# Half of the z gates ahead of the convolution units in a two-block network, step columns inside a quarter of the gates

## The chip, the cores and the metric

The kernel runs on one core of a Trainium2 chip. The metric is the device time of one launch in microseconds (us).

## What is computed

A network of two blocks over 1024 tokens of 1024 channels. The first (a linear recurrence beside differential attention, then an expert-choice feed-forward layer) is not touched. The second block begins with one wide projection; cut to what matters here:

```
h = layer_norm(x, ln_emb_g, ln_emb_b)
proj = einsum('bld,de->ble', h, w_in)
xs, z, bm, cm, dt_raw, glu, cgate = split(proj, ...)   # 1024, 1024, 256, 256, 16, 2048, 1024 columns
xbc = silu(causal_depthwise_conv(concat([xs, bm, cm]), ssm_conv_w, ssm_conv_b))       # 4 taps
dt = softplus(dt_raw + dt_bias)
y = ssd_chunked(xh, dt, a, bm_c, cm_c) + d_skip * xh
yz = y * silu(z)                                       # then a grouped rms norm: y_ssm
u = glu[..., :1024] * sigmoid(glu[..., 1024:])
u = causal_depthwise_conv(u, conf_conv_w, conf_conv_b)                                # 31 taps
u = silu(layer_norm(u, conf_ln_g, conf_ln_b))
y_conf = u * silu(cgate)
out = concat([y_ssm, y_conf]) @ w_out + b_out          # and two more norms and a gate
```

## The kernel before

Products are made at more than one pass: each operand is split into a high and a low part, and `mm3` (line 135) issues three matmuls, high by high, high by low, low by high. The contraction runs over eight tiles of 128 channels. A projection (`proj`) gives 128 columns for all 1024 tokens, with the weights stationary: 48 matmuls of 512 tokens. The gates z are wanted with tokens on partitions: `z(q)` makes 256 columns at a time for two token blocks of 128, with the tokens stationary, in 192 matmuls of 256 columns a quarter, and stores silu(z) in device memory.

A scheduler of the framework fixes the order of each engine's instructions when the program is built; the Python order of the stages, the buffers of the pools and the lists `later` and `bgq` steer it. `after()`, called at the end of every projection, runs what was put on `later`: the turning (transposing) of a finished tile on TensorE, or the sums of the step columns. `bg(us)` takes that much VectorE work from `bgq`, the queue of convolution taps: 20 of a tile's 31 taps go to VectorE (line 1295, accumulator in PSUM), the rest to ScalarE (products, line 1291) and GpSimd (additions, line 1292).

The second block's stages come in this order: the layer norm of x, read from device memory after the first block (`normed`), four token blocks at a time; their transposes (`turned`), between the matmuls of the first gated linear unit (`first`); `glu` 1; `bc` 0 (B, with its turns, line 1357); `glu` 2; `dts`, the projection of the 16 step columns (48 matmuls with 16 rows of output, line 1402 turns them); `bc` 1; `glu` 3 to 7 with `xs` 0 to 3 between; z quarters 0 to 2; the eight convolution gates (cgate); z quarter 3 with the first part of the state-space stage. `steps` makes softplus of the step columns: a chain of 15 operations on 128x128 tiles on VectorE (`log1p`, lines 179 to 188, then lines 1411 and 1416), and the matmuls of `sums` (lines 1423, 1424), which wait for it, are put three calls of `after` later:

```
later.append(lambda: later.append(lambda: later.append(sums)))
```

The norm over channels takes the mean `mu` (channel sum by TensorE, line 1488, then line 1492) late in z quarter 2; squares are summed (lines 1497, 1505); `deviation` (lines 1509 to 1515) follows behind gate 1; `gated(j)` (lines 1497, 1519, 1521) is run two gates behind the gate that it needs.

## Time and profile before

| | us |
|---|---|
| median of 3 runs (2226.93 to 2230.64) | 2229.42 |
| the profiled execution | 2233.63 |
| its span, first to last instruction | 2231.9 |
| TensorE busy | 2077.4 (93%) |
| VectorE busy | 1767.3 (79%) |
| ScalarE busy | 1200.1 (54%) |
| GpSimd busy | 515.8 (23%) |

Busy time is the time in which an engine had an instruction under way; matmuls are pipelined, so their durations overlap, and what a matmul costs is read from the distance of two starts. PE is TensorE (PEld its weight loads), DVE VectorE, ACT ScalarE, POOL GpSimd, SP SyncE, whose queue issues most transfers. All times in the rows are in us from the start of the span. The mean granted clock of TensorE is 0.964 of its full speed.

### The profile page before, as it was taken

Reading aid. Unit: us, or ns where it says so; the run is one execution under the profiler, and the core shown is the slowest. Engines: PE = TensorE matmul, PEld = TensorE weight load, DVE = VectorE, ACT = ScalarE, POOL = GpSimd, SP = SyncE. Lnnn points to the kernel's source line nnn. Section 1 sums busy time; section 2 is a strip of 40 time slices with the busy share of each in tenths; the row PEclk is TensorE's granted clock in tenths of the full one; section 3 lists DMA queues with packets and bytes.
Section 4 is the critical chain, followed back from the end, with each engine's and each line's share of the span. In section 5 each row is a group of like instructions: output and inputs, shape, how many; then the busy total and the mean of one; then the engine's idle time right before and its main releaser. Section 6 shows DMA issues by size and latency. Waiting matters only on the chain.

```text
span 2231.9 us, 27077 instructions
## 1 busy us (share of the span) xinstructions
PE 2077.4 (93%) x10214; PEld 1717.7 (77%) x10214; DVE 1767.3 (79%) x2389; ACT 1200.1 (54%) x1427; POOL 515.8 (23%) x254
## 2 busy tenths in 40 slices
PE   6989899989979999999998689989999999998997
PEld 6768678978868888878877477767889887776885
DVE  7587859976878999989977648999993748877676
ACT  5563839982327777766766447544543346544111
POOL 0133310000021121201101018766774210003000
PEclk9999999999979999999999899989999999999998
DMA  8444456127578999999998321133434458556211
GB/s 271 141 148 127 123 142 121 55 91 253 191 283 327 387 389 386 378 384 356 383 335 292 112 60 49 57 104 114 123 114 151 169 180 284 180 199 215 76 67 66
DMA packets 232802, 439.67 MB, mean 197 GB/s; under 512 B 46656, under 2 KB 134976, under 8 KB 232544
## 3 DMA queue, kind: packets, MB, share of 16 engines
q1 hardware_dynamic: 217184, 396.00, 51.3%
q0 software_dynamic: 9728, 35.66, 5.1%
q10 hardware_dynamic: 5760, 6.29, 0.8%
q8 instruction: 80, 1.31, 0.2%
q14 instruction: 50, 0.41, 0.1%
HBM read 370.74 MB, written 67.16 MB: 196 GB/s over the span
## 4 chain that ended last, share of the span: by engine, by line
PE 52%; issue 7%; DVE 6%; DMA 3%; ACT 2%; POOL 1%; SPq 0%; DVEq 0%; POOLq 0%; ACTq 0%
PE big L142 16%; PE big L139 16%; PE big L140 16%; PE tr L1012 1%; DVE tr L1295 1%; DMA x1d<-y,idx 1%; ACT wH L129 1%; PE tr L997 1%; DMA ptd<-rs 1%; DMA wr<-in_w_out_dram 1%; PE big L1357 1%; PE tr L1768 1%; POOL acc L1292 0%; DVE wL L133 0%; DVE aL L133 0%
## 5 line engine op out<-in xcount | busy, mean ns | idle before, releaser
L129 ACT CAST wH<-wr 128x2048 fp32r<-128x2048 f32 (+2 forms) x267 | 443.1, 1667 | 258.7 <-PE big L142 154.1
L133 DVE TENSOR_TENSOR wL<-wr,wH 128x2048 fp32r<-128x2048 f32 (+1 forms) x206 | 454.4, 2216 | 72.4 <-ACT wH L129 71.7
L139 PE MATMUL big<-hH,wH 128*128 128x512 f32 (+1 forms) x720 | 285.8, 402 | 11.3 <-ACT B L410 4.7
L140 PE MATMUL big<-hL,wH 128*128 128x512 f32 (+1 forms) x720 | 286.7, 400 | 6.5 <-DVE hL L326 5.7
L142 PE MATMUL big<-hH,wL 128*128 128x512 f32 (+1 forms) x720 | 228.1, 395 | 0.0
L1295 DVE SCALAR_TENSOR_TENSOR tr<-u,cols,tr 128x1024 f32<-128x1024 f32 x160 | 205.8, 1286 | 12.1 <-ACT tr L1283 8.5
L133 POOL TENSOR_TENSOR wL<-wr,wH 128x1024 fp32r<-128x1024 f32 (+2 forms) x62 | 154.7, 2501 | 253.0 <-ACT wH L129 232.7
L1292 POOL TENSOR_TENSOR acc<-acc,tmp 128x1024 f32<-128x1024 f32 x72 | 174.1, 2419 | 37.1 <-ACT tmp L1291 31.7
L139 PEld LDWEIGHTS big<-hH,wH 128*128 128x128 f32 (+1 forms) x720 | 137.3, 191 | 44.6 <-ACT B L410 5.1
L140 PEld LDWEIGHTS big<-hL,wH 128*128 128x128 f32 (+1 forms) x720 | 137.6, 191 | 38.1 <-DVE hL L326 6.8
L142 PEld LDWEIGHTS big<-hH,wL 128*128 128x128 f32 (+1 forms) x720 | 136.6, 190 | 30.8
L139 PE MATMUL big<-hH,aH 128*128 128x512 f32 x384 | 154.6, 403 | 5.3 <-ACT aH L129 2.3
L139 PE MATMUL big<-wH,0H 128*128 128x512 f32 x384 | 151.9, 395 | 3.8 <-ACT 0H L129 3.8
L139 PE MATMUL big<-wH,hH 128*128 128x256 f32 (+1 forms) x448 | 150.0, 336 | 4.6 <-ACT wH L129 2.1
L140 PE MATMUL big<-hL,aH 128*128 128x512 f32 x384 | 152.7, 398 | 1.0 <-DVE hL L1562 1.0
L140 PE MATMUL big<-wL,0H 128*128 128x512 f32 x384 | 153.1, 399 | 0.0
L140 PE MATMUL big<-wL,1H 128*128 128x512 f32 x384 | 152.3, 397 | 0.0
L139 PE MATMUL big<-wH,1H 128*128 128x512 f32 x384 | 151.1, 394 | 1.1 <-ACT 1H L129 1.1
L140 PE MATMUL big<-wL,hH 128*128 128x256 f32 (+1 forms) x448 | 149.4, 334 | 0.9 <-POOL wL L133 0.9
L142 PE MATMUL big<-wH,hL 128*128 128x256 f32 (+1 forms) x448 | 148.7, 332 | 0.0
L142 PE MATMUL big<-wH,0L 128*128 128x512 f32 x384 | 120.3, 395 | 4.8 <-DVE 0L L133 4.7
L142 PE MATMUL big<-hH,aL 128*128 128x512 f32 x384 | 122.9, 398 | 1.8 <-DVE aL L133 1.5
(534 smaller groups left out, 4470.4 us busy)
## 6 DMA issues: line engine op xcount, KB each, us to landing
wr<-in_w_dram SPq DMA_DIRECT2D x192, 1024.0 KB
wr<-in_w_in_dram SPq DMA_DIRECT2D x48, 512.0 KB
wm<-in_w_mod_dram SPq DMA_DIRECT2D x32, 512.0 KB
wm<-in_w_mod_dram SPq DMA_DIRECT2D x8, 1024.0 KB
wr<-in_w_in_dram SPq DMA_DIRECT2D x32, 256.0 KB
u<-ucd SPq DMA_DIRECT2D x16, 512.0 KB
wr<-in_w_out_dram SPq DMA_DIRECT2D x14, 512.0 KB
hL<-in_x_dram SPq DMA_DIRECT2D x8, 512.0 KB
```

The source lines that it names most:

```text
L129: self.high = nc.scalar.copy(h, src)
L133: (le or nc.vector).tensor_sub(l, src, h)
L139: mm(o, aH, bH, start=start, stop=False)
L140: mm(o, aH, bL, start=False, stop=False)
L142: mm(o, aL, bH, start=False, stop=stop)
L997: self.turn = nc.tensor.matmul(pr[:, 0:4], oh[:, b], tk[:, e, b], start=b == 0, stop=b == NB - 1)
L1012: self.turned = nc.tensor.transpose(pt[:, k * P:(k + 1) * P], src[:, k * P:(k + 1) * P], self.ident)
L1292: nc.gpsimd.tensor_add(part[0], part[0], tmp)
L1295: nc.vector.scalar_tensor_tensor(acc[0], u[:, t:t + S], w(t), acc[0], op0=ALU.mult, op1=ALU.add)
L1357: nc.tensor.transpose(pt[:, b], src[:, b * P:(b + 1) * P], self.ident)
L1768: nc.tensor.transpose(pt[:, k * P:(k + 1) * P], src[:, k * P:(k + 1) * P], self.ident)
```

## The change

The second block begins with the first half of z instead of the first unit: its 512 gate columns are made for two token blocks at a time (`tokens`, `gates`), 48 matmuls of 512 columns each, and the layer norm and the transposes go by two token blocks too (`normed`, `turned`); the square root there is made on VectorE alone (`rsqrt_v`). `glu(0)` is a unit like the others. `dts` makes z's third quarter, 256 columns, with the 16 step columns beside it, in 192 matmuls of 272 columns; `steps` has no turning any more, its bias is added as a row, and `sums` is put one call of `after` later instead of three. Behind `glu(7)` come gates 0 to 2 in place of z quarters 0 to 2; `mu` follows gate 2, `deviation` gate 4, and gates 4 and 5 have buffers of their own. The last z quarter stays where it was.

```diff
-        self.w0 = self.c_weights(W[:, 2576:2576 + P], W[:, 3600:3600 + P], le=self.nc.vector)
-        self.x0 = self.normed(0, [self.ct(i // 2) for i in range(4)])
-
-    def normed(self, half, xts):
-
-        nc, sm = self.nc, self.csm
+        self.w0 = self.z_weights(W[:, 1024:1536], le=self.nc.vector)
+        ln = lambda n, *w: self.cst.tile([P, NB, *w], F, name="ln" + n)
+        self.lnv, self.lnr, self.lnb = ln("v", 2), ln("r"), ln("b")
+        self.rows = {p: self.normed(p) for p in range(2)}
...
+    def normed(self, p):
+
+        nc, sm, mv = self.nc, self.csm, self.lnv
+        xts = [self.ct(p % 2) for _ in range(2)]
         for i, xt in enumerate(xts):
-            b = half * 4 + i
+            b = p * 2 + i
             self.xload = nc.sync.dma_start(xt, self.x1d[b * P:(b + 1) * P, :])
-        mv = sm.tile([P, 4, 2], F, name="mv")
-        r = sm.tile([P, 4], F, name="cer")
-        nm = sm.tile([P, 4], F, name="nm", bufs=1)
-        for p in range(2):
-            for i in (2 * p, 2 * p + 1):
-                bs = sm.tile([P, 2, 6], F, name="bs")
-                for q in range(2):
-                    nc.vector.bn_stats(bs[:, q], xts[i][:, q * 512:(q + 1) * 512])
-                nc.vector.bn_aggr(mv[:, i], bs.rearrange("p a b -> p (a b)"))
-            ps = slice(2 * p, 2 * p + 2)
-            self.rsqrt(sm, mv[:, ps, 1], 2, 1.0, LN_EPS, "ce", r[:, ps])
-            if half == 0:
-                nc.vector.scalar_tensor_tensor(nm[:, ps], mv[:, ps, 0], -1.0, r[:, ps], op0=ALU.mult, op1=ALU.mult)
-            for i in (2 * p, 2 * p + 1):
-                if half == 0 and i % 2 == 0:
-                    nc.scalar.activation(xts[i], xts[i], AF.Identity, bias=nm[:, i:i + 1], scale=r[:, i:i + 1])
-                else:
-                    self.last = nc.vector.tensor_scalar(xts[i], xts[i], mv[:, i, 0:1], r[:, i:i + 1], op0=ALU.subtract, op1=ALU.mult)
-        return xts, mv, r
+        bs = slice(2 * p, 2 * p + 2)
+        for i, xt in enumerate(xts):
+            st = sm.tile([P, 2, 6], F, name="bs")
+            for q in range(2):
+                nc.vector.bn_stats(st[:, q], xt[:, q * 512:(q + 1) * 512])
+            nc.vector.bn_aggr(mv[:, 2 * p + i], st.rearrange("p a b -> p (a b)"))
+        r = self.lnr[:, bs]
+        nc.vector.tensor_copy(r, self.rsqrt_v(sm, mv[:, bs, 1], 2, 1.0, LN_EPS, "ce"))
+        nc.vector.scalar_tensor_tensor(self.lnb[:, bs], mv[:, bs, 0], -1.0, r, op0=ALU.mult, op1=ALU.mult)
+        b = 2 * p
+        nc.scalar.activation(xts[0], xts[0], AF.Identity, bias=self.lnb[:, b:b + 1], scale=r[:, 0:1])
+        nc.vector.tensor_scalar(xts[1], xts[1], mv[:, b + 1, 0:1], r[:, 1:2], op0=ALU.subtract, op1=ALU.mult)
+        return xts
+
+    def z_weights(self, *aps, le=None):
+
+        nc, wp = self.nc, self.cwp
+        ws = []
+        for h in range(4):
+            wr = self.cwr.tile([P, 2, 512], F, name="wr")
+            n = 0
+            for ap in aps:
+                n += ap.shape[1]
+                nc.sync.dma_start(wr[:, :, n - ap.shape[1]:n], ap[h * 256:(h + 1) * 256].rearrange("(k p) n -> p k n", p=P))
+            wH = wp.tile([P, 2, 512], R, name="wH")
+            wL = wp.tile([P, 2, 512], R, name="wL")
+            self.split(wH[:, :, 0:n], wL[:, :, 0:n], wr[:, :, 0:n], le or nc.gpsimd)
+            ws += [(wH[:, k, 0:n], wL[:, k, 0:n]) for k in range(2)]
+        return ws
...
+        def turned(p, xts):
+
+            ts = slice(p * 256, p * 256 + 256)
+            for k4 in range(2):
+                pt = (pq.tile([P, 4, 256], F, name="big") if k4 else pt1.tile([P, 4, 256], F, name="tr"))
+                for q in range(4):
+                    k = k4 * 4 + q
+                    for i in range(2):
                         nc.tensor.transpose(pt[:, q, i * P:(i + 1) * P], xts[i][:, k * P:(k + 1) * P], self.ident)
+                for q in range(4):
+                    k = k4 * 4 + q
                     g, b = self.col("ln_emb_g", k), self.col("ln_emb_b", k)
-                    nc.scalar.activation(hH[k][:, hs], pt[:, q], AF.Identity, bias=b, scale=g)
-                    if half:
+                    nc.scalar.activation(hH[k][:, ts], pt[:, q], AF.Identity, bias=b, scale=g)
+                    if p == 0 or q == 3:
                         nc.vector.tensor_scalar(pt[:, q], pt[:, q], g, b, op0=ALU.mult, op1=ALU.add)
                     else:
-                        self.evac = nc.scalar.activation(pt[:, q], pt[:, q], AF.Identity, bias=b, scale=g)
-                    nc.vector.tensor_sub(hL[k][:, hs], pt[:, q], hH[k][:, hs])
+                        nc.scalar.activation(pt[:, q], pt[:, q], AF.Identity, bias=b, scale=g)
+                    nc.vector.tensor_sub(hL[k][:, ts], pt[:, q], hH[k][:, ts])
...
+        def tokens(p, w, mid=None):
+
+            ps = pq.tile([P, 2, 512], F, name="big")
+            n = w[0][0].shape[1]
+            for kt in range(KT):
+                if kt == 4 and mid:
+                    mid()
+                for i in range(2):
+                    sl = slice((p * 2 + i) * P, (p * 2 + i + 1) * P)
+                    self.mm3([ps[:, i, 0:n]], hH[kt][:, sl], hL[kt][:, sl], [w[kt][0]], [w[kt][1]], kt == 0, kt == KT - 1)
+            after()
+            return ps
+
+        def gates(p, ps, c0, n):
+
+            o = st.tile([P, 2, n], F, name="t2", bufs=3)
+            nc.scalar.activation(o, ps[:, :, 0:n], AF.Silu)
+            nc.sync.dma_start(self.szd[p * 256:(p + 1) * 256, c0:c0 + n].rearrange("(a p) c -> p a c", p=P), o)
...
+            turned(0, self.rows.pop(0))
+
+            def mid(p):
+                if p < 3:
+                    turned(p + 1, self.rows.pop(p + 1))
+                if p < 2:
+                    self.rows[p + 2] = self.normed(p + 2)
+
+            for p in range(4):
+                gates(p, tokens(p, w, lambda: mid(p)), 0, 512)
...
-            ps = proj(weights(W[:, 2560:2576]), 0, NE)
-            raw = st.tile([NE, S], F, name="t2", bufs=3)
-            nc.scalar.activation(raw, ps[0:NE, :], AF.Identity, bias=self.col("dt_bias")[0:NE])
-            later.append(lambda: steps(raw))
...
+            db = sm.tile([P, NE], F, name="db")
+            self.row_bcast(db, "dt_bias")
+            w = self.z_weights(W[:, 1536:1792], W[:, 2560:2576])
             cut = Cut(ct(1))
             v = cut.tile([P, P], F, "v")
-            nc.scalar.copy(v, pt[:, 0])
+            for p in range(4):
+                ps = tokens(p, w)
+                gates(p, ps, 512, 256)
+                nc.vector.tensor_add(v[:, p * 32:p * 32 + 32].rearrange("p (b h) -> p b h", b=2), ps[:, :, 256:272],
+                                     db[:, None, :].to_broadcast([P, 2, NE]))
+                self.bg(10.0)
+            steps(cut, v)
...
-            later.append(lambda: later.append(lambda: later.append(sums)))
-
-        def z_weights(q):
-            return weights(W[:, 1024 + q * 256:1280 + q * 256])
-
-        def z(q, w=None, mid={}):
-
-            cs = slice(q * 256, (q + 1) * 256)
-            w = w or z_weights(q)
+            later.append(sums)
...
+        def cgate(j):
+            if j % 2 == 0:
+                self.wc = weights(W[:, 4624 + j * P:4880 + j * P])
+            ps = proj(self.wc, j % 2)
+            os[j] = self.cp.tile([P, S], F, name="os", bufs=2) if j in (4, 5) else ct(j % 2)
+            nc.scalar.activation(os[j], ps, AF.Silu)
+
+        first(self.w0)
...
-        z(0)
-        z(1)
+        cgate(0)
+        cgate(1)
...
-        z(2, mid={ZM: [lambda: nc.scalar.activation(mu, chan_sum(s1, mu), AF.Copy, scale=1.0 / D)]})
+        cgate(2)
+        nc.scalar.activation(mu, chan_sum(s1, mu), AF.Copy, scale=1.0 / D)
...
-        os = {}
-        for j in range(KT):
-            if j % 2 == 0:
-                w = weights(W[:, 4624 + j * P:4880 + j * P])
-            ps = proj(w, j % 2)
-            os[j] = ct(j % 2)
-            nc.scalar.activation(os[j], ps, AF.Silu)
-            if j == 1:
+        for j in range(3, KT):
+            cgate(j)
+            if j == 4:
                 deviation()
-            if j > 1:
-                gated(j - 2, os.pop(j - 2))
-        w = z_weights(3)
-        for j in (6, 7):
+            if j >= 4:
+                for i in range(j - 1 if j > 4 else 0, j):
+                    gated(i, os.pop(i))
+        w = weights(W[:, 1792:2048])
+        for j in sorted(os):
             gated(j, os.pop(j))
         es1.close()
         self.c2_es.close()
         es.close()
         self.ssd_open()
         mid, first = self.ssd_first(pq)
-        z(3, w, mid)
+        z(w, mid)
```

The order of TensorE around the sums of the step columns, before (L1423, L1424; `t` is the product of step and decay, `hH` and `hL` the split tokens, `wH` and `wL` the split weights):

```order
L140 MATMUL big<-hL_10518,wH 128x512
L139 MATMUL big<-hH_10510,wH 128x512
L140 MATMUL big<-hL_10518,wH 128x512
L142 MATMUL big<-hH_10510,wL 128x512 x2
L1423 MATMUL big<-t_11475,iota_10325 128x128
L1424 MATMUL big<-t_11475,ones 128x128
L139 MATMUL big<-hH_10503,wH 128x512
```

The same place now (lines are one less or some ten more):

```order
L138 MATMUL big<-wH,hH_10521 128x272
L139 MATMUL big<-wL,hH_10521 128x272
L141 MATMUL big<-wH,hL_10529 128x272
L138 MATMUL big<-hH_10514,wH 128x512
L139 MATMUL big<-hL_10522,wH 128x512
...
L139 MATMUL big<-hL_10529,wH 128x512
L141 MATMUL big<-hH_10521,wL 128x512 x2
L1434 MATMUL big<-t_11655,iota_10325 128x128
L1435 MATMUL big<-t_11655,ones 128x128
L138 MATMUL big<-hH_10514,wH 128x512
```

Between the turned step columns and the sums 144 matmuls stood (three projections); now 48 (one) stand between the quarter's last matmul and the sums.

VectorE in the first part of the step chain, before (L179 to L187 are the chain, L1295 the taps, L1350 those of the short convolution, L1298 the end of a tile's convolution):

```order
L179 TENSOR_SCALAR t_11475<-t_11475 128x128
L1350 SCALAR_TENSOR_TENSOR t_11499<-big,cols,t_11499 128x1021
L1295 SCALAR_TENSOR_TENSOR tr<-u,cols,tr 128x1024
L180 RECIPROCAL t_11475<-t_11475 128x128
L1298 TENSOR_TENSOR acc<-tr,acc 128x1024
L1339 MEMSET u 128x30
L181 TENSOR_TENSOR t_11475<-t_11475 128x128
L183 TENSOR_TENSOR t_11475<-t_11475 128x128
L185 TENSOR_SCALAR t_11475<-t_11475 128x128
```

The same place now (L178 to L186 are the chain, L1314 the taps, L1410 the added bias of the last two token blocks):

```order
L1410 TENSOR_TENSOR t_11655<-big,db 128x32
L1314 SCALAR_TENSOR_TENSOR tr<-u,cols,tr 128x1024
L178 TENSOR_SCALAR t_11655<-t_11655 128x128
L1314 SCALAR_TENSOR_TENSOR tr<-u,cols,tr 128x1024
L179 RECIPROCAL t_11655<-t_11655 128x128
L1314 SCALAR_TENSOR_TENSOR tr<-u,cols,tr 128x1024
L180 TENSOR_TENSOR t_11655<-t_11655 128x128
L1314 SCALAR_TENSOR_TENSOR tr<-u,cols,tr 128x1024
L182 TENSOR_TENSOR t_11655<-t_11655 128x128
```

One tap stands between two operations of the chain here; 12 other operations in all stand in it up to the product that the sums wait for, and behind it no tap is left ahead of the next unit's product.

TensorE at the start of the last z quarter, before (`seg` is the first product of the state-space part):

```order
L140 MATMUL big<-hL_10518,wH 128x512
L142 MATMUL big<-hH_10510,wL 128x512 x2
L1651 MATMUL seg<-CT,BT 128x128
L139 MATMUL big<-wH,hH_10503 128x256
L140 MATMUL big<-wL,hH_10503 128x256
```

The same product now:

```order
L141 MATMUL big<-wH,hL_10529 128x256
L138 MATMUL big<-wH,hH_10514 128x256
L1659 MATMUL seg<-CT,BT 128x128
L139 MATMUL big<-wL,hH_10514 128x256
L141 MATMUL big<-wH,hL_10522 128x256
```

It stood ahead of the quarter's first matmul; now 145 of the quarter's 192 stand ahead of it.

## Rows read from the trace of the kernel before

**Rows 1.** The page: busy us (share of the span) and instructions of each engine.

```profile
PE 2077.4 (93%) x10214; PEld 1717.7 (77%) x10214; DVE 1767.3 (79%) x2389; ACT 1200.1 (54%) x1427; POOL 515.8 (23%) x254
```

**Rows 2.** Table by stretch, in us: busy PE, PEld, DVE, ACT, POOL; clock, DMA.

```profile
1350.00:1690.00 340.00, 323.24 (x1570) 268.20 (x1569) 316.54 (x268) 176.00 (x174) 252.74 (x108) 0.97 0.33 97
```

**Rows 3.** Timeline of TensorE: start us, us, line, tile, [idle before <-releaser].

```profile
1254.65 0.39 PE L140 MATMUL big<-wL,1H 128*128 128x512 f32 x1
...
1260.54 0.39 PE L140 MATMUL big<-wL,1H 128*128 128x512 f32 x1
1260.77 0.61 PE L142 MATMUL big<-wH,1L 128*128 128x512 f32 x2
1284.10 0.69 PE L1223 MATMUL tr<-ident,t 128*128 128x128 f32 x2 [22.71 <-ACT t L1143]
```

**Rows 4.** Waits of TensorE, 1340 to 1660: us in total, times, longest.

```profile
PE big L1357 <- ACT t L1351: 9.6, 4, 3.1
```

**Rows 5.** Timeline of TensorE, at the sums of the step columns.

```profile
1454.63 0.76 PE L1423 MATMUL big<-t,iota 128*128 128x128 f32 x2 [7.18 <-DVE t L1416]
```

**Rows 6.** Timeline of VectorE, from the convolution's end to the state-space part.

```profile
1689.92 1.22 DVE L1298 TENSOR_TENSOR acc<-tr,acc 128x1024 f32<-128x1024 f32 x1 [1.78 <-POOL acc L1292]
1721.36 3.48 DVE L1497 TENSOR_TENSOR u<-u,tr 128x1024 f32<-128x1024 f32 x3 [30.21 <-ACT tr L1492]
...
1749.52 1.22 DVE L1509 TENSOR_SCALAR s<-big 128x1024 f32<-128x1024 f32 x1 [5.69 <-PE big L1488]
...
1764.26 2.35 DVE L1519 TENSOR_TENSOR u<-u,r 128x1024 f32<-128x1024 f32 x2
...
1788.39 1.23 DVE L1521 TENSOR_TENSOR u<-u,t 128x1024 f32<-128x1024 f32 x1 [0.18 <-ACT u L1520]
...
1815.97 1.23 DVE L1521 TENSOR_TENSOR u<-u,t 128x1024 f32<-128x1024 f32 x1 [9.65 <-ACT t L1530]
...
1846.53 1.23 DVE L1696 TENSOR_TENSOR big<-big,xs 128x1024 f32<-128x1024 f32 x1
```

**Rows 7.** Table by stretch, in the last z quarter (columns as in rows 2).

```profile
1820.00:1830.00 10.00, 10.00 (x82) 9.83 (x81) 3.82 (x6) 8.51 (x22) 0.00 (x0) 1.00 1.00 368
1830.00:1840.00 10.00, 10.00 (x82) 9.83 (x82) 4.85 (x8) 7.01 (x18) 0.53 (x1) 1.00 0.50 170
```

**Rows 8.** Timeline of TensorE, in the third z quarter (256 columns).

```profile
1694.82 0.28 PE L142 MATMUL big<-wH,hL 128*128 128x256 f32 x1
...
1697.70 0.28 PE L142 MATMUL big<-wH,hL 128*128 128x256 f32 x1
```

**Rows 9.** Groups by form, TensorE, 1385 to 1415: busy us, mean ns, idle before.

```profile
L139 PE MATMUL big<-hH,wH 128*16 128x512 f32 x16 | 6.3, 392 | 0.0
...
L1402 PE MATMUL big<-ident,t 16*128 16x16 f32 x8 | 0.7, 211 | 0.0
```

**Rows 10.** Timeline of VectorE, first statistics of the layer norm.

```profile
1274.45 1.29 DVE L1135 BATCH_NORM_STATS2 bs<-t 128x6 f32<-128x512 f32 x2 [9.56 <-DMA t<-x1d]
```

**Rows 11.** Line 1357, turns of B: ns min/median/max, first and last start.

```profile
L1357 PEld LDWEIGHTS big<-ident,BT x16: 138/140/143, 1368.0 to 1380.7; 128*128 128x128 f32 x16
```

**Rows 12.** Timeline of VectorE, in the step chain.

```profile
1426.46 2.38 DVE L183 TENSOR_TENSOR t<-t 128x128 f32<-128x128 f32 x1
...
1431.21 7.33 DVE L187 SCALAR_TENSOR_TENSOR t<-t 128x128 f32<-128x128 f32 x3
...
1442.25 0.28 DVE L187 SCALAR_TENSOR_TENSOR t<-t 128x128 f32<-128x128 f32 x1
```

**Rows 13.** Timeline of GpSimd, in the same stretch.

```profile
1431.06 7.34 POOL L1292 TENSOR_TENSOR acc<-acc,tmp 128x1024 f32<-128x1024 f32 x3
1449.63 2.35 POOL L1292 TENSOR_TENSOR acc<-acc,tmp 128x1024 f32<-128x1024 f32 x1 [11.23 <-ACT tmp L1291]
```

**Rows 14.** Timeline of ScalarE, the last unit's first activation.

```profile
1655.69 1.11 ACT L1335 ACTIVATE t<-big,hb 128x1024 f32<-128x1024 f32 x1
```

More of the change, by code (lines that the diff above doesn't have):

```diff
@@ L41 @@
 EDGE = 352
-ZM = 3
 _COLS = [
@@ L1251, in proj @@
             return ps
-        def first(w):
-            x0, *n0 = self.x0
-            turned(0, x0)
-            with tc.issue_after(self.last.ins):
-                x1, *n1 = self.normed(1, [self.cf.tile([P, S + 30], F, name="u", bufs=3)[:, 0:D] if i < 3 else
-                                          self.cf.tile([P, S], F, name="acc", bufs=3) for i in range(4)])
-            pss = []
-            for half in range(2):
-                hs = slice(half * 512, half * 512 + 512)
-                if half:
-                    turned(1, x1)
-                    for i, (mv, r) in enumerate((n0, n1)):
-                        nc.vector.tensor_copy(self.lnm[:, i * 4:i * 4 + 4], mv[:, :, 0])
-                        nc.vector.tensor_copy(self.lnr[:, i * 4:i * 4 + 4], r)
-                    nc.vector.scalar_tensor_tensor(self.lnb, self.lnm, -1.0, self.lnr, op0=ALU.mult, op1=ALU.mult)
-                pss.append(pq.tile([P, S], F, name="big"))
-                for kt in range(KT):
-                    for j in range(2):
-                        self.mm3([pss[half][:, j * 512:j * 512 + 512]], w[kt][0][:, j * P:(j + 1) * P],
-                                 w[kt][1][:, j * P:(j + 1) * P], [hH[kt][:, hs]], [hL[kt][:, hs]], kt == 0, kt == KT - 1)
-            return pss
@@ L1316, in glu @@
         def glu(j):
-            if j == 1:
-                with tc.issue_after(self.xload.ins), tc.issue_after(self.evac.ins):
-                    w = glu_weights(j)
-            else:
-                w = glu_weights(j) if j else self.w0
-            halves = [(p, slice(h * 512, h * 512 + 512)) for h, p in enumerate(first(w))] if j == 0 else ()
-            pa = None if halves else proj(w, 0)
+            w = glu_weights(j)
+            pa = proj(w, 0)
             hb = sm.tile([P, 2], F, name="hb", bufs=2)
@@ L1327, in glu @@
             a = ct(0)
-            if not halves:
-                nc.scalar.activation(a, pa, AF.Identity, bias=hb[:, 0:1], scale=0.5)
-            for p, hs in halves:
-                nc.scalar.activation(a[:, hs], p[:, 0:512], AF.Identity, bias=hb[:, 0:1], scale=0.5)
-            pg = None if halves else proj(w, 1)
+            nc.scalar.activation(a, pa, AF.Identity, bias=hb[:, 0:1], scale=0.5)
+            pg = proj(w, 1)
             g = ct(1)
-            if not halves:
-                nc.scalar.activation(g, pg, AF.Tanh, bias=hb[:, 1:2], scale=0.5)
-            for p, hs in halves:
-                nc.scalar.activation(g[:, hs], p[:, 512:S], AF.Tanh, bias=hb[:, 1:2], scale=0.5)
+            nc.scalar.activation(g, pg, AF.Tanh, bias=hb[:, 1:2], scale=0.5)
             u = cf.tile([P, S + 30], F, name="u", bufs=3)
@@ L1477, in in_proj2 @@
         glu(7)
-        z(0)
-        z(1)
+        cgate(0)
+        cgate(1)
         self.bg(1e9)
         esf.close()
-        cp = pool(name="cp", bufs=1)
+        cp = self.cp = pool(name="cp", bufs=1)
         def chan_sum(s, ps):
```

39 lines of the change are left out of this document (10 added, 29 removed).

## The prediction

> **What bounds the kernel now.** I read the page first: TensorE is busy 2077 of 2232 us, VectorE 1767 [rows 1]. Only the second block changes, so I looked at its stretches. From 1350 to 1690, where the projections of the gated linear units run beside the depthwise convolution, TensorE is busy 323 of 340 us and VectorE 317 [rows 2]: two engines that are both nearly full, so a saving on one can turn into a wait on the other. The timeline of TensorE gives the start: the first block's last matmul begins at 1260.8, the second block's first transposes at 1284.1, after 22.7 us of idle time [rows 3]. The waits of TensorE between 1340 and 1660 name above all the turning of B and xs tiles (9.6 us) [rows 4] and, in the timeline, one wait of 7.2 us for VectorE, ahead of the cumulative sums of the step columns [rows 5]. Behind the last unit comes the layer norm over channels: mean, deviation, eight gated tiles, a chain of VectorE and ScalarE [rows 6] under which TensorE computes the convolution gates. At the end stands the last quarter of z [rows 7].
>
> **Prices.** A matmul of 512 columns starts 0.227 us after the one before (5.89 us for 26 steps [rows 3]); one of 256 columns 0.120 us (2.88 us for 24 steps [rows 8]). For 272 columns no row exists; I take 0.127, on the line between the two, with 0.120 and 0.136 (the price of 256 columns times 272/256) as bounds. A step-column matmul, 16 rows out, costs as much as a full one: 16 by 392 ns of the same 512 columns [rows 9].
>
> **TensorE's work.** z's first half was 384 matmuls of 256 columns (46.1 us) and is 192 of 512 (43.6): -2.5. The step columns' own projection, 48 of 512 columns, goes (-10.9), and with it eight small transposes (-0.7 [rows 9]). z's third quarter grows from 256 to 272 columns: +1.3 (0 to 3). Sum: -12.8 us. "TensorE: Matmul & The Clock Gate" of the Trainium skill, section Back-to-back issue gap, gives N/2.4 + 2.5 ns for an isolated warm matmul, 216 and 109 ns for these widths; by that the sum would be about -10. It also gives 131 ns for 512 columns in a sustained stream, which the 227 ns here do not bear out. The rows decide.
>
> Against this stand the waits. I follow the path by waypoints, before and after, in times of the profiled execution.
>
> **A, start.** Before, VectorE's first statistics wait until 1274.5 for x [rows 10], and transposes follow at 1284.1. Now two token blocks are enough, and the square root is done on VectorE without ScalarE; but x stands in SyncE's queue behind four weight loads, the rows dsk, db and al and six loads of unit weights, and the first pair's normalisation behind the other blocks' statistics. I take +1.5, bounds -2 and +4. From the first transposes to the first turn of B (1368.0 [rows 11]) were 288 matmuls (65.3), 64 transposes (8) and 10.6 of loss: the four-block halves wait for each other's evacuation. Now 480 matmuls (109) stand there, and pairs of token blocks overlap: I take a loss of 4, bounds 0 and 10.6. First turn of B: 1285.6 + 109 + 8 + 4 = 1406.6.
>
> **B, third quarter.** 96 matmuls of glu(2) (21.8), two turns (2.2), 192 of 272 columns (24.4): its end Q is 1455.
>
> **C, the step chain.** Softplus and products are 15 dependent VectorE operations on 128x128, in the order between 12 others (taps and short-convolution taps, some 1.2 us each, 14.5). Before, 144 matmuls stood ahead of the sums, 32.7 us of cover; now 48, 10.9 us. What an operation of the chain costs depends on GpSimd: while GpSimd adds, three take 7.33 us and one 2.38; while it idles (11.2 us ahead of 1449.6), one takes 0.28 [rows 12, 13]. So 15 operations take 4.2 (GpSimd idle) to 18.8 us (as before). With 14.5 and 2.8 of latency after Q the sums begin 21.5 to 36.1 after Q; I take 28.8, nearer to the upper rows because GpSimd still has its convolution share there. Sums: S = 1484, and TensorE arrives at Q + 10.9 = 1466: it waits 18 us (10.6 to 25), against 7.2 before [rows 5].
>
> **D, to the end of the last unit.** Before, from 1454.6 to 1655.7 [rows 5, 14]: 201.1 us, of which 16 projections are 174.2, the eight turns 8.8, and 18 are lost, to VectorE above all. Now 19 projections (206.9) and the turns (8.8). VectorE used the wait of C to clear its taps, so I take a loss of 10, bounds 0 and 18: 1484 + 225.7 = 1710.
>
> **E, to the mean.** Before, 528 matmuls of 256 columns and 2.2 us to 1721.3. Now 187 of 512 (42.4) and 3: 1755. The convolution ends 34 us after the last unit before (1689.9 [rows 6]); the cover here is 45, so it is not late.
>
> **F, mean to the last gated tile.** Centring and squares 22.6, channel sum 2.3 (5.7 before: only 53 matmuls now stand between the two sums), deviation 14.7, eight gated tiles. Six took from 1764.3 to 1789.6, 4.2 each, before the last two waited for gates (9.7 us alone [rows 6]); the gates are now early, but the eight tiles stand closer: 33.9. The last ends at 1829, before 1817.2: +12.
>
> **G, to the state-space part.** From the last gated tile to the first product with x (1846.5 [rows 6]) 29.3 us passed, in which TensorE ran the last z quarter while VectorE was busy 3.8 and 4.9 of 10 us and ScalarE 8.5 and 7.0 [rows 7]. Now TensorE has 197 x 0.227 + 192 x 0.120 = 68 us after the mean and ends z at about 1823, ahead of the gated tiles; 145 of its 192 matmuls lie before the first segment product. What remains of the 29.3 is ScalarE's and VectorE's own work, 4 to 9 us less. So the shift of all that follows is +3 to +8; I take **+6**. Everything behind G is the same work in the same order.
>
> **The sum.** 2233.63 + 6 = 2239.6 for the profiled execution, which stands 4.2 above the median: 2235.4 on the scale of the runs. A saving of 12.8 on TensorE is eaten by 11 of longer wait at C and by VectorE's chain at F, whose cover the moved convolution gates no longer give.
>
> **Rivals.**
> 1. TensorE stays the bound (faster). GpSimd idles through most of the chain, so the wait at C is 10.6 (+3.4), and F is hidden or shorter since all gates are ready. The loss at A falls by 6.6 and the work by 12.8, with +1.5 for the start: -14.5, 2214.9. For it: the gates no longer end F's waits. Against it: the cover before the sums falls by 21.8 us, and F's chain is VectorE's own. It decides if the gated tiles end before TensorE's last z matmul.
> 2. VectorE falls behind (much slower). The chain runs wholly under GpSimd (+7 at C); then VectorE has no taps left until the next unit's product, which needs three projections (32.7) after the sums, and is full from there, so the loss at D stays at 18 (+8): +21, 2250. For it: VectorE's 317 of 340. Against it: the taps done during the wait. By "GPSIMD Engine Reference" of the Trainium skill, section Specifications, GpSimd shares its SBUF interfaces with VectorE, in contention with VectorE instructions that have two SBUF inputs: by that rule alone every chain operation that meets an addition of GpSimd's is slow, and this is the case to expect; the trace agrees as to the price (2.4 against 0.28), and shows GpSimd idle for the second half of the chain.
> 3. Losses and gains cancel: C at 12 instead of 18 brings -6, or G gives back all 12: 0, 2229.4.
> 4. The program does not move: excluded by the order rows, which show the step projection gone and the sums 48 matmuls behind the quarter.
>
> **How the numbers follow.** 0.2% (4.5 us) is about what a measurement of this kernel can tell from no change. Forecast 0.29 and rival 2 0.16: slower 0.45. Rival 3: same 0.25. Rival 1 and a part of it (a gain of 5 to 15): faster 0.30. The forecast's own bounds: C -7 to +7, A's loss -4 to +6.6, D -10 to +8, the start -3.5 to +2.5, not all at once: 2222 to 2249. The range reaches to rival 1 below, with some 4 us more for a start at its lower bound, and past rival 2 above by its start at the upper one: 2207 to 2256.
>
> **What would show it.** In the changed profile: steps of 0.227 us in z's first half, no 16-row matmuls; first transposes near 1285.6 and first turn of B near 1407 (A); one wait of TensorE for VectorE's step product of 10 to 25 us at about 1466 (C), with chain operations of 0.3 us where GpSimd idles and 2.4 where not; the last unit's Tanh near 1710 (D); the mean near 1755 (E); the last gated tile near 1829 (F); the first product with x 3 to 8 us later than 1846.5 (G). If the wait at C is under 8 us the forecast is wrong towards rival 1; if the first product with x comes before 1842, G is wrong too.

## The result and the profile after

The changed kernel takes 2257.49 us (median of 4, 2254.8 to 2259.02) against 2230.03 of the kernel before (2226.93 to 2233.27): ratio 1.0127, 95% interval 1.0115 to 1.0139. It is slower by 27.5 us; the forecast was 6 us slower, with a range that ended at 2256. The two profiled executions are 22.5 us apart (spans 2254.4 and 2231.9): that of before (2233.63) was slower than each of the four timed runs, that of the change (2256.08) the second fastest of its four.

TensorE is busy 8 us less (2069.2 us, 2077.4 before [rows 1]; 12.8 were forecast from the distances of starts, and a matmul of 272 columns starts 0.126 us after the one before, 0.127 forecast). Its timeline at the start, at the first turn of B, at the end of the third quarter and at the sums, to be read against [rows 3, 5, 11]:

```profile
1287.87 0.47 PE L1231 MATMUL tr<-ident,t 128*128 128x128 f32 x1 [25.97 <-ACT t L1140]
...
1411.28 0.93 PE L1365 MATMUL big<-ident,BT 128*128 128x128 f32 x7
...
1458.79 0.29 PE L141 MATMUL big<-wH,hL 128*128 128x272 f32 x1
...
1469.38 0.61 PE L141 MATMUL big<-hH,wL 128*128 128x512 f32 x2
1487.85 0.77 PE L1434 MATMUL big<-t,iota 128*128 128x128 f32 x2 [17.85 <-DVE t L1427]
```

The quarter ends at 1459, TensorE comes to the sums at about 1470 and waits 17.85 us for VectorE's step product; 18 were forecast, 7.2 stood before. VectorE's timeline in the step chain, and from the end of the convolution on, against [rows 6, 12]:

```profile
1466.05 1.71 DVE L180 TENSOR_TENSOR t<-t 128x128 f32<-128x128 f32 x1
...
1476.05 0.28 DVE L186 SCALAR_TENSOR_TENSOR t<-t 128x128 f32<-128x128 f32 x1
...
1748.15 1.22 DVE L1317 TENSOR_TENSOR acc<-tr,acc 128x1024 f32<-128x1024 f32 x1 [1.47 <-POOL acc L1311]
1760.17 2.35 DVE L1509 TENSOR_TENSOR u<-u,tr 128x1024 f32<-128x1024 f32 x2 [10.80 <-ACT tr L1504]
...
1784.19 1.23 DVE L1521 TENSOR_SCALAR s<-big 128x1024 f32<-128x1024 f32 x1 [3.88 <-PE big L1499]
...
1801.36 1.21 DVE L1531 TENSOR_TENSOR u<-u,r 128x1024 f32<-128x1024 f32 x1
...
1814.24 1.22 DVE L1509 TENSOR_TENSOR u<-u,tr 128x1024 f32<-128x1024 f32 x1 [4.45 <-DMA u<-ucd]
...
1835.95 1.23 DVE L1533 TENSOR_TENSOR u<-u,t 128x1024 f32<-128x1024 f32 x1 [1.31 <-ACT u L1532]
...
1868.84 1.23 DVE L1704 TENSOR_TENSOR big<-big,xs 128x1024 f32<-128x1024 f32 x1
```

GpSimd in the step chain, against [rows 13]:

```profile
1469.98 4.81 POOL L1311 TENSOR_TENSOR acc<-acc,tmp 128x1024 f32<-128x1024 f32 x2
1483.90 2.35 POOL L1322 TENSOR_TENSOR s<-s,acc 128x1024 f32<-128x1024 f32 x1 [9.11 <-DVE u L1347]
```

Up to 1474.8 us operations of the chain took 1.0 to 1.7 us beside GpSimd's work, in the idle time behind it 0.28. The reciprocal is apart: 0.94 us here and 0.95 with GpSimd idle (e9_quarter_start, below). The last unit's first activation on ScalarE, against [rows 14]:

```profile
1715.54 1.11 ACT L1345 ACTIVATE t<-big,hb 128x1024 f32<-128x1024 f32 x1
```

And all engines (busy PE, PEld, DVE, ACT, POOL; granted clock, DMA share, GB/s) from the last gated tile to the first product with x, against [rows 7], where TensorE was busy throughout at a clock of 1.00:

```profile
1837.20:1868.80 31.60, 18.14 (x82) 12.29 (x80) 18.92 (x26) 25.02 (x53) 2.62 (x5) 0.73 0.99 360
```

The forecast's waypoints beside the traces, in us from the start of the span:

| | before | forecast | now |
|---|---|---|---|
| first transposes | 1284.1 | 1285.6 | 1287.9 |
| first turn of B | 1368.0 | 1406.6 | 1411.0 |
| sums | 1454.6 | 1484 | 1487.9 |
| last unit's activation | 1655.7 | 1710 | 1715.5 |
| first centred tile | 1721.4 | 1755 | 1760.2 |
| end of the last gated tile | 1817.2 | 1829 | 1837.2 |
| first product with x | 1846.5 | 1852 | 1868.8 |
| end of the span | 2231.9 | | 2254.4 |

From the first product to the end both take the same, 385.4 and 385.6 us. All of the difference lies ahead of it.

### The profile page after: what moved, and what is told of

It reads as the page before. It is cut to its first block, busy times and chain, and to the rows that moved or that the text cites. A ratio compares the mean times of both kernels' runs of the same rounds, so it can differ in the third digit from the quotient of the medians.

```text
span 2254.4 us, 26622 instructions
## 1 busy us (share of the span) xinstructions
PE 2069.2 (92%) x9966; PEld 1706.0 (76%) x9966; DVE 1762.5 (78%) x2440; ACT 1206.7 (54%) x1441; POOL 514.7 (23%) x252
## 4 chain that ended last, share of the span: by engine, by line
PE 51%; DVE 8%; issue 6%; DMA 4%; ACT 3%; POOL 0%; SPq 0%; DVEq 0%; ACTq 0%; POOLq 0%
PE big L141 16%; PE big L138 15%; PE big L139 15%; PE tr L1011 1%; DMA wr<-in_w_out_dram 1%; ACT wH L128 1%; DMA u<-ucd 1%; PE tr L996 1%; DVE wL L132 1%; DMA ptd<-rs 1%; PE tr L1776 0%; PE big L1365 0%; DVE tr L1314 0%; DMA t<-x1d 0%; DMA rs<-x1d 0%
## 5 line engine op out<-in xcount | busy, mean ns | idle before, releaser
L138 PE MATMUL big<-hH,wH 128*128 128x512 f32 x704 | 278.7, 398 | 6.7 <-ACT B L409 4.7
L139 PE MATMUL big<-hL,wH 128*128 128x512 f32 x704 | 278.8, 396 | 6.1 <-DVE hL L325 6.1
L1314 DVE SCALAR_TENSOR_TENSOR tr<-u,cols,tr 128x1024 f32<-128x1024 f32 x160 | 205.8, 1286 | 18.7 <-ACT tr L1302 15.0
L141 PE MATMUL big<-hH,wL 128*128 128x512 f32 x704 | 219.3, 393 | 0.0
L138 PEld LDWEIGHTS big<-hH,wH 128*128 128x128 f32 x704 | 134.2, 191 | 36.4 <-ACT B L409 5.1
L139 PEld LDWEIGHTS big<-hL,wH 128*128 128x128 f32 x704 | 135.0, 192 | 35.4 <-DVE hL L325 7.0
L141 PEld LDWEIGHTS big<-hH,wL 128*128 128x128 f32 x704 | 134.0, 190 | 28.5
L139 PE MATMUL big<-hL,aH 128*128 128x512 f32 x384 | 152.2, 397 | 1.3 <-DVE hL L1570 1.2
L139 PE MATMUL big<-wL,0H 128*128 128x512 f32 x384 | 153.3, 399 | 0.0
L138 PE MATMUL big<-wH,hH 128*128 128x512 f32 (+2 forms) x384 | 139.0, 363 | 3.9 <-ACT wH L128 2.2
L141 PE MATMUL big<-wH,hL 128*128 128x512 f32 (+2 forms) x384 | 137.6, 359 | 3.0 <-DVE hL L1240 3.0
L139 PE MATMUL big<-wL,hH 128*128 128x512 f32 (+2 forms) x384 | 138.2, 360 | 0.6 <-POOL wL L132 0.6
```

The lines of the kernel that those rows point to most:

```text
L138: mm(o, aH, bH, start=start, stop=False)
L139: mm(o, aH, bL, start=False, stop=False)
L141: mm(o, aL, bH, start=False, stop=stop)
L1314: nc.vector.scalar_tensor_tensor(acc[0], u[:, t:t + S], w(t), acc[0], op0=ALU.mult, op1=ALU.add)
```

## The experiments

Two questions: is the longer wait ahead of the sums lost for good, and what bounds the stretch behind the last unit? Theory: a **chain** of dependent work (convolution of the last unit, mean, squares, deviation, gated tiles, decays) ends last there. Rival: **TensorE** does, as before. The edits are against the changed kernel unless another is named. In the table, "behind" is the time from the last unit's activation to the first product with x, in the profiled execution; each ratio is to the kernel before, run beside it.

| | median us | ratio (95%) | last unit | first product | behind |
|---|---|---|---|---|---|
| before | 2230.0 | | 1655.7 | 1846.5 | 190.8 |
| the change | 2257.5 | 1.0127 (1.0115 to 1.0139) | 1715.5 | 1868.8 | 153.3 |
| e1_sums_later | 2236.7 | 1.0036 (1.0022 to 1.0050) | 1695.8 | 1848.9 | 153.1 |
| e8_before_sums_early | 2249.4 | 1.0089 (1.0067 to 1.0110) | 1671.0 | 1861.9 | 190.9 |
| e2_gates_cut | 2262.2 | 1.0147 (1.0130 to 1.0164) | 1715.6 | 1874.5 | 158.9 |
| e15_quarter_twice | 2261.2 | 1.0153 (1.0131 to 1.0174) | 1716.5 | 1873.5 | 157.0 |
| e4_squares_cut | 2257.9 | 1.0129 (1.0112 to 1.0146) | 1716.8 | 1870.3 | 153.5 |
| e10_more_u | 2258.2 | 1.0141 (1.0125 to 1.0156) | 1723.0 | 1872.1 | 149.1 |
| e3_start_only | 2241.8 | 1.0057 (1.0040 to 1.0074) | 1686.6 | 1854.9 | 168.3 |
| e5_start_timed | 2224.9 | 0.9994 (0.9983 to 1.0005) | 1684.0 | 1834.8 | 150.8 |
| e7_timed_sbuf | 2229.7 | 1.0005 (0.9994 to 1.0015) | 1688.2 | 1845.9 | 157.7 |
| e6_mu_sbuf | 2266.8 | 1.0176 (1.0152 to 1.0200) | 1715.3 | 1876.1 | 160.8 |
| e11_wout_ahead | 2266.3 | 1.0168 (1.0142 to 1.0193) | 1719.4 | 1877.7 | 158.4 |
| e12_later_ahead | 2248.2 | 1.0090 (1.0064 to 1.0115) | 1698.1 | 1855.9 | 157.8 |
| e13_no_low | 2255.6 | 1.0128 (1.0111 to 1.0145) | 1718.0 | 1870.1 | 152.2 |
| e14_two_loads | 2263.6 | 1.0153 (1.0130 to 1.0176) | 1715.8 | 1874.8 | 158.9 |
| e9_quarter_start | 2210.6 | 0.9921 (0.9907 to 0.9935) | 1658.4 | 1826.8 | 168.5 |

**The wait ahead of the sums.** The sums go back to three calls later:

```diff
-            later.append(sums)
+            later.append(lambda: later.append(lambda: later.append(sums)))
```

> The changed kernel with the sums of the step columns put three calls of after() later, as before. TensorE's wait of 17.9 us ahead of the sums should fall to under 3 us. If the longer wait is a cost of its own, all that follows comes earlier by it: 12 to 17 us less than the changed kernel. If VectorE uses the wait to clear taps that would otherwise hold TensorE up later, the wait only moves: 0 to 5 us less.

TensorE's timeline at the sums of this kernel:

```profile
1489.19 0.38 PE L1434 MATMUL big<-t,iota 128*128 128x128 f32 x2
```

No wait is left, and the time falls by 20.8 us, more than the 12 to 17 expected; of the 20.0 us between the two profiled executions, 2.2 lie at the start of the second block. The mirror image, the same line turned round in the kernel before:

> The kernel before with one edit, the sums of the step columns one call of after() later instead of three. TensorE's wait ahead of them should grow from 7.2 us to about 29. If a wait of TensorE there is lost for good: 15 to 22 us slower than before. If VectorE's taps done in the wait save TensorE other waits: 0 to 8 us slower.

```profile
1454.84 0.76 PE L1423 MATMUL big<-t,iota 128*128 128x128 f32 x2 [28.06 <-DVE t L1416]
```

The wait grows from 7.2 to 28.1 us, and the time by 20. In the change the wait is lost in full: from the first transposes to the last unit's activation its profiled execution takes 427.7 us and that of e1_sums_later 410.1, less by about the 17.85 of the wait. In the kernel before the medians say the same, but the two profiled executions differ by less there, 385.8 against 371.6 us, 14 for 21 more of wait. So the taps that VectorE does in the wait save TensorE nothing later in the change, and at most a third of it in the kernel before.

**Who bounds the stretch behind the last unit.** Less of TensorE's work there:

```diff
-            ps = proj(self.wc, j % 2)
+            ps = proj(self.wc, j % 2, n=KT if j < 5 else 1)
```

> The changed kernel with convolution gates 5 to 7 over one of the eight contraction tiles only (the rest of their products is left out), 126 matmuls or 28.6 us of TensorE's work after the mean. Theory: behind the last unit the chain of VectorE (convolution, mean, squares, deviation, gated tiles) sets the end, so 0 to 3 us less. Rival, TensorE is still the bound there: 20 to 28 us less.

And more of it, the last z quarter's products made twice:

```diff
-                    for kt in range(KT):
+                    for kt in [*range(KT)] * 2:
```

> The changed kernel with the matmuls of the last z quarter made twice (the second pass starts the sums anew, so the result is the same): 192 matmuls of 256 columns, 23 us of TensorE, more at the place where TensorE stands idle for half of the time at a granted clock of 0.73. If TensorE's idle time there is free and its low clock costs nothing: within 4 us of the changed kernel. If the low clock stretches the steps between segment products: 2 to 8 us less than the changed kernel although TensorE does more, with the clock at 1.00 in that stretch. If TensorE is the bound there: 15 to 23 us more.

First the stretch from the last unit's activation to the first product with x, before and then in the change (columns as above):

```profile
1655.70:1846.50 190.80, 190.80 (x1212) 172.36 (x1210) 109.08 (x91) 84.42 (x116) 66.64 (x36) 1.00 0.48 162
```

```profile
1715.50:1868.80 153.30, 130.62 (x640) 106.39 (x638) 106.95 (x94) 77.93 (x106) 50.28 (x30) 0.91 0.52 182
```

Before, TensorE is busy all of the time; in the change it is not. The engines of the changed kernel and then of e2_gates_cut from 1757 to 1870:

```profile
1757.00:1870.00 113.00, 89.12 (x457) 72.04 (x455) 79.91 (x74) 59.60 (x91) 14.54 (x15) 0.88 0.60 212
```

```profile
1757.00:1870.00 113.00, 63.42 (x327) 51.24 (x326) 79.67 (x74) 59.30 (x86) 13.92 (x15) 0.74 0.63 222
```

TensorE is busy 25.7 us less, and the kernel is 4.7 us slower, not faster: outside both expectations, by a difference little beyond the scatter whose cause was not settled. With 23 us more (e15_quarter_twice) it is 3.7 slower. TensorE's work does not bound this stretch any more. What its clock costs there is not shown. With the repeated matmuls the granted clock is 1.00 from 1840 to 1870 instead of 0.71, and the first product is no earlier; but TensorE is then busy all of these 30 us, and what the clock gave may have gone to the added matmuls. In the change itself the chain of work that ended last holds 1.23 us of TensorE between 1837 and 1869, so by that chain the clock had little to give.

```profile
1857.86 1.23 PE seg L1674 x2
```

The engines from 1840 to 1870 in the change, then in e15_quarter_twice:

```profile
1840.00:1870.00 30.00, 15.34 (x59) 9.49 (x57) 18.14 (x24) 26.22 (x57) 0.09 (x1) 0.71 1.03 377
```

```profile
1840.00:1870.00 30.00, 30.00 (x233) 28.56 (x232) 12.89 (x18) 17.47 (x37) 0.00 (x0) 1.00 0.68 246
```

Pieces of the chain, next. Six additions fewer on VectorE (`if j > 6` in place of `if j > 0` in the sum of squares), and a fourth buffer for the tiles read back (for which one of the five buffers of the first block's weights, line 241, goes):

> The changed kernel with six of the seven additions of squares left out (the variance is wrong by that), some 7 us of VectorE's work between mean and deviation, nothing of TensorE's. Theory, VectorE's chain sets the end: 5 to 8 us less than the changed kernel. Rival, TensorE sets it: 0 to 1 us less.

> The changed kernel with four buffers instead of three for the convolution's tiles that are read back for the mean and the gated tiles. If the reloads through three buffers pace the two passes (in e4_squares_cut the first pass took no less time with six additions fewer): 3 to 8 us less than the changed kernel. If VectorE's own operations pace them: 0 to 2 us less.

Neither changes the median. With the additions gone, the pass from mean to deviation still takes 18.2 us (20.2 in the change): VectorE now waits for reloads, 6 us in all. With four buffers the time from the first to the last centred tile falls from 72.0 to 63.7, what follows up to the first product takes 4.2 more, and the 4.2 us that stay do not show in the median. They may have gone to the buffer taken from the first block: its second block begins 4.6 us later than the change's (1292.5 against 1287.9), later than in any other run. The buffer alone was not tried. In both runs the chain passes from one resource to the next, and each alone had only a few us to give.

**Only the start.** Step columns, sums and third quarter as before; the quarter and gate 0 fill TensorE behind the last unit, the mean follows gate 1:

```diff
-        cgate(0)
-        cgate(1)
+        z(2)
+        cgate(0)
         self.bg(1e9)
...
-        cgate(2)
+        cgate(1)
         nc.scalar.activation(mu, chan_sum(s1, mu), AF.Copy, scale=1.0 / D)
```

> Only the first half of z is moved to the start; step columns, their sums and the third quarter are as before (the quarter behind the last unit), the mean follows gate 1. Theory: 43.6 us moved ahead of the last unit, against about 48 us that the stretch behind it could give up before VectorE's chain bounds it, so close to the kernel before: minus 5 to plus 6 us against before, 22 to 32 less than the changed kernel. Rival, the new start itself costs: within 8 us of the changed kernel.

2241.8, 12.5 above before: better than the change by 15.7, outside what was expected. Its deviation's sum stands behind gate 4 on TensorE, 34.4 us after the mean's. The next kernel changes only that: `proj` calls a function after half of its contraction, for the mean in gate 1 and for the deviation in gate 3.

```diff
+                if kt == 4 and mid:
+                    mid()
```

> As e3_start_only, but the mean's channel sum is put into the middle of gate 1 and the deviation's into the middle of gate 3, so that neither stands long behind gates on TensorE. Theory, a chain from the last unit's convolution over mean, squares, deviation and gated tiles to the first segment product sets the end: in e3_start_only the deviation's sum came 34.4 us after the mean's where 23.2 do in the changed kernel, so 8 to 20 us less than e3_start_only, 2222 to 2234. Rival, the chain is not what ends last: within 3 us of e3_start_only.

17 us come back: 2224.9, no different from before. The waits of TensorE from 1684 to 1835 in this kernel, and from 1716 to 1869 in the change (us in total, times, longest; L1499 is the deviation's sum):

```profile
PE seg L1663 <- DVE u L1515: 3.4, 1, 3.4
```

```profile
PE big L1499 <- DVE s L1517: 9.2, 1, 9.2
PE seg L1674 <- DVE M L1676: 5.0, 2, 3.8
PE seg L1659 <- DVE M L1676: 4.1, 2, 2.1
PE seg L1674 <- ACT VL L1673: 2.6, 2, 1.9
```

Where the two small sums are placed in TensorE's order matters, since VectorE's chain hangs on them. But of the 17.4 us by which the two profiled executions differ behind the last unit, only 8 lie ahead of the end of the last gated tile; the other 9 lie in the stretch behind it (34.2 to 24.8 us), where neither sum stands.

**The last stretch, which did not shrink in the change.** From the last gated tile to the first product I had forecast some 23 us; it is 31.7. Six kernels looked for one cause, and five of them came out slower, outside both expectations. The mean in SBUF instead of PSUM (the two on-chip memories in which the kernel keeps its tiles), which frees the PSUM bank that the first segment product takes over, in the change and in e5_start_timed:

```diff
-        nc.scalar.activation(mu, chan_sum(s1, mu), AF.Copy, scale=1.0 / D)
+        mus = cp.tile([P, S], F, name="mus")
+        nc.scalar.activation(mus, chan_sum(s1, mu), AF.Copy, scale=1.0 / D)
```

> The changed kernel with the mean in SBUF: its PSUM bank is free after the channel sum, so the first segment product need not wait for the last centred tile. If that bank is what holds the state-space stage back: 5 to 15 us less than the changed kernel, with the first segment product tens of us earlier. If the buffers of the gated tiles in SBUF hold it back as well: 0 to 3 us less, with only the first segment product earlier.

> Both edits, e5_start_timed with the mean in SBUF: the same difference to e5_start_timed as e6_mu_sbuf has to the changed kernel, 5 to 15 us or 0 to 3.

```profile
1770.72 0.38 PE L1660 MATMUL seg<-CT,BT 128*128 128x128 f32 x2
1782.01 1.22 PE L1499 MATMUL big<-s,ones 128*128 128x512 f32 x1 [10.91 <-DVE s L1518]
```

The first segment product comes 63.5 us earlier (1834.2 in the change), and the kernel is 9 us slower; e7_timed_sbuf is 5 slower than e5_start_timed, at the edge of the scatter. Why slower was not settled. The bank alone isn't the cause. Next the buffers of the output weights, which lie on those of the gated tiles. The chain of work that ended last in the change passes through them (start, us, what):

```profile
1837.47 3.29 DMA ycd<-u
...
1840.78 8.88 DMA wr<-in_w_out_dram
```

```diff
-        self.raw2 = pool(name="w1r", bufs=4)
         st = pool(name="sst", bufs=2)
+        self.raw2 = pool(name="w1r", bufs=4)
```

> The changed kernel with one edit behind the gated tiles: the four buffers through which the output weights are read are placed behind the state-space stage's own tiles in SBUF, not on the buffers of the gated tiles, so that their first loads need not wait until the last gated tile is stored. If that hand-over (store 3.3 us, load 8.9 us, then the casts in ScalarE's order ahead of the first product with x) paces the 33 us between the last gated tile and the first product: 4 to 10 us less than the changed kernel. If the decays' own chain paces it: 0 to 2 us less.

> e1_sums_later with the same edit: if the two causes are apart from each other, the same difference as between e11_wout_ahead and the changed kernel, on top of e1_sums_later's: 2227 to 2233 or 2235 to 2237.

Both are slower, by 9 and 12 us: the scheduler then put the casts of these weights and other work ahead of the first product on VectorE. Then ScalarE's work, and six of the eight loads:

> The changed kernel in which the low part of the step products is left out of the decays of the first two chunks: 32 of ScalarE's 128x128 operations (10 us) and 8 of TensorE's matmuls go, between the last gated tile and the first product with x and just behind it. If ScalarE's own work paces that stretch (it is busy 25.0 of its 31.6 us): 4 to 9 us less than the changed kernel, and the stretch from the last gated tile's multiplication (33 us now) under 29. If loads of the output weights or VectorE's order pace it: 0 to 2 us less.

> The changed kernel in which only two of the eight 512 KB tiles of the output weights' second half are loaded and the other six products use these two again (six loads of the output weights are left out, all casts and matmuls stay): 3.1 MB less of the 11.9 MB that move between the last gated tile and the first product with x. If transfers pace that stretch (the DMA share of its time is 0.99): 5 to 9 us less than the changed kernel, and the stretch from the last gated tile's multiplication under 28 us instead of 33. If the order on VectorE or ScalarE paces it: 0 to 2 us less.

Without the low parts the engines from the last gated tile to the first product:

```profile
1839.71:1870.11 30.40, 16.18 (x75) 11.36 (x73) 18.60 (x27) 18.21 (x28) 2.63 (x5) 0.72 0.99 359
```

ScalarE has 7 us less to do, and the stretch is 1.3 us shorter. ScalarE now waits for transfers instead, of the output weights and of tiles read back:

```profile
1852.07 1.04 ACT L128 CAST hH<-wr 128x1024 fp32r<-128x1024 f32 x1 [3.40 <-DMA wr<-in_w_out_dram]
...
1863.31 1.04 ACT L128 CAST aH<-yc 128x1024 fp32r<-128x1024 f32 x1 [1.87 <-DMA yc<-ycd]
```

With two loads the stretch is longer and the kernel 6 us slower (the eight casts moved ahead of the later decays), so this run doesn't tell what the loads cost: it took away transfers and changed the order as well.

In one kernel the stretch did shrink: 24.8 us in e5_start_timed, against 30 to 37 in the others that move z to the start (29.3 in e9_quarter_start, below). There most of the last z quarter stands in the stretch, TensorE is busy throughout at a clock of 0.98, and ScalarE casts the first four tiles of output weights in one piece without a wait, where the change casts them one by one between the decays and waits for the first. The engines of e5_start_timed, its casts, and the first cast of the change:

```profile
1810.00:1834.80 24.80, 24.69 (x182) 22.95 (x181) 15.88 (x25) 19.73 (x46) 2.64 (x5) 0.98 0.98 356
```

```profile
1825.56 3.88 ACT L128 CAST hH<-wr 128x1024 fp32r<-128x1024 f32 x4
```

```profile
1849.68 1.04 ACT L128 CAST hH<-wr 128x1024 fp32r<-128x1024 f32 x1 [2.85 <-DMA wr<-in_w_out_dram]
```

Whether the order, the clock or the loads make these 7 us was not tried one by one. What paces the stretch stays open; only e13_no_low took away one resource and left the order mostly as it was.

**A version that beats both.** From e5_start_timed: the start makes z's first quarter with the step columns (272 columns) instead of z's half, `dts` is gone, the sums stand three calls behind, z quarters 1 and 2 follow the last unit, the mean sits in quarter 2 and the deviation in gate 1.

```diff
-        self.w0 = self.z_weights(W[:, 1024:1536], le=self.nc.vector)
+        self.w0 = self.z_weights(W[:, 1024:1280], W[:, 2560:2576], le=self.nc.vector)
...
-        dts()
...
-        z(2)
-        cgate(0)
+        z(1)
         self.bg(1e9)
...
-        cgate(1, lambda: nc.scalar.activation(mu, chan_sum(s1, mu), AF.Copy, scale=1.0 / D))
+        z(2, mid={3: [lambda: nc.scalar.activation(mu, chan_sum(s1, mu), AF.Copy, scale=1.0 / D)]})
```

> From e5_start_timed: the start makes z's first quarter with the step columns beside it (272 columns) instead of z's first half, the step columns' own projection is gone, the sums stand three calls of after() behind, and z quarters 1 and 2 fill TensorE behind the last unit, the mean in the last token blocks of quarter 2, the deviation in gate 1. TensorE's work is about 10 us less than before and 24 us instead of 44 move ahead of the last unit. Theory, the end is the later of TensorE's work and the chain behind the last unit, and the former here: 6 to 12 us less than before, 2216 to 2222. Rival, the step chain at the start, among the layer norm's work on VectorE, holds TensorE up: within 3 us of before or slower.

2210.6 us, 0.9921 of before (0.9907 to 0.9935) and 46.9 us under the change; 17 under before, 5 more than expected. TensorE at its sums (no wait), the last of the step chain's products on VectorE, and TensorE's longest waits from 1260 to 1850:

```profile
1365.93 0.38 PE L1428 MATMUL big<-t,iota 128*128 128x128 f32 x2
```

```profile
1345.46 0.29 DVE L1421 SCALAR_TENSOR_TENSOR t<-dt,al 128x128 f32<-128x128 f32 x1
```

```profile
PE tr L1231 <- ACT t L1140: 24.3, 1, 24.3
PE big L1374 <- ACT t L1368: 8.6, 4, 2.2
PE big L141 <- DVE hL L1240: 6.0, 6, 3.6
PE seg L1670 <- DVE M L1672: 1.6, 1, 1.6
```

The wait ahead of the sums is gone. The chain has no taps between its operations there and ends 11 us behind the quarter, and three projections stand ahead of the sums. Only 24 us of work move ahead of the last unit, so TensorE remains the bound behind it, busy 168.0 of 168.4 us:

```profile
1658.40:1826.80 168.40, 167.98 (x1020) 149.23 (x1018) 110.55 (x90) 79.59 (x110) 59.36 (x34) 1.00 0.50 171
```

From the first transposes to the last unit's activation both kernels take 371.6 us, although 13.5 us more of TensorE's work stand there now (24.4 less 10.9). The 7.2 us of the wait account for half of that; the rest was not taken apart.

## Why the prediction was wrong

Right were the sign, the price of the wide matmuls, and **C** almost to the digit: the wait (18 forecast, 17.85 measured), its cause (cover of one projection instead of three) and the price of the chain (28.8 us from the quarter's end to the sums, as forecast). The Trainium skill, in "GPSIMD Engine Reference", Specifications, names contention of GpSimd with VectorE instructions that run in a 2-port perf mode or have two SBUF inputs. The trace agrees as far as it goes: beside GpSimd's work operations with two inputs took 1.3 to 1.7 us, without it 0.28; those with one input took 1.0 and 1.2 beside it, and in which mode they ran the rows don't tell. Rival 2, at 2250, came nearest in number, but not by its mechanism: it needed a wait of 25 us at C and a loss of 18 at D, which was 12.

Wrong was the size, by 21.5 us. The step that failed is **G**, and with it the sum. Behind the last unit the forecast had 142 us to the first product with x (1710 to 1852); it is 153.3, and 149 to 161 in all kernels that keep the change's order there. Of these 11, 8.7 are G: I took 4 to 9 us off a stretch of 29.3 because the z quarter would be done earlier; with the quarter it took 29.3, with most of the quarter done ahead 31.7, so the quarter was not what it waited for. e5_start_timed says the same from the other side: with most of the quarter in it the stretch took 24.8. What it waits for in the change stays open. Another 3 are F (77.0 us for 74; one gated tile waited 4.5 us for a reload). The last unit itself comes 5.5 late: 2.3 at the first transposes, which came between 1284.9 and 1289.8 in the runs that have the same code up to there, 2.1 of loss in A (6.1 for 4), the rest in D. That makes 16 between the profiled executions; the remaining 5 are the place of the two profiled executions among their runs (3.6 above its median before, 1.4 below it now).

What I did not see is why the sum had to come out so. Before, TensorE was the bound behind the last unit, with 190.8 us; where TensorE idles there, the chain took 149 to 161. So by my estimate about 40 us could be moved ahead of the last unit at no loss; e5_start_timed, which moves 43.6, came out even. The change moves 57 net (43.6 and 24.4, less 10.9) and adds 11 of wait. I had the terms (F and G say that VectorE's chain ends last) and never added them up to one length. The closing sentence of the sum sets the 12.8 us saved on TensorE against the waits, though the sum itself goes by the waypoints: 10.9 of them are saved ahead of the last unit and are in the 57, and behind it e2_gates_cut and e15_quarter_twice, with 25.7 us less and 23 us more of TensorE, show no gain from doing less.

## What to carry to other kernels

Before moving work ahead of a point, take the length of the chain of dependent work behind it, with no waits for the busiest engine: only the difference to the present length can be moved. A wait of the bounding engine on a chain of small operations was lost in full in the changed kernel here, and for two thirds or more in the one before, so keep the cover (three projections) when the order around it is rewritten, or start the chain where its engine has little else in its order. Small sums on which a chain hangs belong into the middle of a long product, not behind it: 17 us here, of which 8 lie on that chain and the rest in the stretch behind it.

## What the runs showed of the hardware

The start of the second block scatters: in ten kernels with the same code up to there the first transposes came at 1284.9 to 1289.8 us, so that two profiled executions can differ by 5 us before the second block has begun. And a subtraction on 128x1024 that takes 1.2 us otherwise took 3.42 us in e6_mu_sbuf beside GpSimd's work on the weights (line 132), when its second operand had moved from PSUM to SBUF:

```profile
1798.50 3.42 DVE L1510 TENSOR_TENSOR u<-u,mus 128x1024 f32<-128x1024 f32 x1
```

```profile
1798.37 2.47 POOL L132 TENSOR_TENSOR wL<-wr,wH 128x1024 fp32r<-128x1024 f32 x1 [3.05 <-ACT wH L128]
```
